# Hybrid encoder trunk on one core: the mixer's VectorE work in source order with paced convolution taps, and two projections with split weights in three passes

## The chip, the cores and the metric

The kernel runs on one core of a Trainium2 chip. The metric is the device time of one execution in microseconds; lower is better. Three runs of the kernel before took 1212.13, 1212.34 and 1212.96 us, so the median is 1212.34 us. Six units of the core appear below: TensorE (PE; its weight loads are listed as PEld), VectorE (DVE), ScalarE (ACT), GpSimd (POOL), SyncE (SP), whose queue issues the weight loads, and the DMA engines.

## The reference

Two layers act on 256 tokens of 1024 channels in f32. Each layer is a feed-forward half step, a mixer of two parallel branches (windowed attention and a convolution), a second feed-forward half step, and a gated embedding:

```python
for i in range(DEPTH):
    h = x + 0.5 * swiglu(rms_norm(x, norm_ffn1[i]), w_ffn1_in[i], w_ffn1_out[i])
    u = rms_norm(h, norm_mix[i])
    q, k, v, c, g = jnp.split(u @ w_in[i], splits, axis=-1)
    q = rms_norm(q.reshape(B, S, N_HEADS, HEAD_DIM), q_norm[i])
    k = rms_norm(k.reshape(B, S, KV_HEADS, HEAD_DIM), k_norm[i])
    y_attn = window_attention(q, k, v, sink[i], rel_bias) @ w_attn_out[i]
    c_val, c_gate = jnp.split(c, 2, axis=-1)
    c = c_val * jax.nn.sigmoid(c_gate)
    c = depthwise_conv(c, conv_w[i], conv_b[i])          # 31 taps, 512 channels
    c = jax.nn.silu(layer_norm(c, conv_ln_g[i], conv_ln_b[i]))
    y_conv = c @ w_conv_out[i]
    g_attn, g_conv = jnp.split(jax.nn.sigmoid(g), 2, axis=-1)
    h = h + (g_attn * y_attn + g_conv * y_conv) @ w_o[i]
    h = h + 0.5 * swiglu(rms_norm(h, norm_ffn2[i]), w_ffn2_in[i], w_ffn2_out[i])
    x = h + (p[i] @ w_pe_proj[i]) * jax.nn.sigmoid(rms_norm(h, norm_pe[i]) @ w_pe_gate[i])
```

Attention has 8 query heads and 2 key heads of 64 channels, a sink logit and a bias table; with 256 tokens there are two query blocks of 128.

## The kernel before

**Weights.** All weight matrices are streamed once, through one object, `Weights` (L46 to L139). A *unit* is one or two loads on SP's queue into one of five `raw` buffers of up to 1 MB. A *spec* is a piece of two row blocks of 128 by 512 columns (or four by 256). To prepare a spec, `prep_upto` casts it on ScalarE to `w_hi` (L104), and VectorE subtracts to get `w_lo` (L105): the "split". There are eight buffers of each. `get()` hands out the next spec; before it does, it runs the hooks that `later(n, fn)` has put at this place, and prepares all specs up to seven ahead (`LOOK`).

**Three passes.** A product with a split weight is made by `mm3` (L303) of three float32r matmuls: high by high, high by low, low by high (L310 to L312). A spec that was registered with `raw_spec` isn't split: `get` returns the raw f32 data, and `mm3` issues one f32 matmul (L306), which stands in the trace with two records. Only the attention and convolution outputs, `attn_out` and `conv_out`, are of this kind. While such specs wait, `limit` keeps further loads back.

**Chunks.** `chunk` (L320) runs through the specs of one accumulator in PSUM, of which there are three. After its first `get` it flushes `pending`, the evacuation of the chunk before. Two smaller PSUM tiles serve transposes.

**The mixer's stages**, `mix` from L562, in the order of the source: two chunks of the convolution's input (`conv_in`, 4 `get`s each), queries (4), keys and values (2), four chunks of gates (4 each), `attn_out` (two chunks of 2), `conv_out` (two of 2); then `w_o` in `update` (two of 4). The `get`s of a mixer are numbered from 0 in this text: 8 to 11 are the queries, 12 and 13 keys and values, 14 to 29 the gates, 30 to 33 `attn_out`, 34 to 37 `conv_out`.

- `conv_in` gates its input by a sigmoid (L594, L595); its `turn_c` transposes the result into a padded buffer and then issues the convolution: 31 taps for each of 4 channel blocks. The first tap of a block is on ScalarE (L577), the other 30 are on VectorE (L581), each adding into `y`.
- `head_norms` (L625) normalizes queries and keys: a square on ScalarE, a sum, a reciprocal root of eleven small VectorE instructions (`rsqrt`, L372), and four multiplications (L647). `turn_q` and `turn_k` transpose the results (L672, L697); they are hooks four and three `get`s later.
- The attention itself is a list of hooks among the gates (L768): `scores` (four matmuls, four reductions with bias on VectorE, four exponentials, a reciprocal, four scalings), `attend` (transposes) and `gather` (two matmuls; the second head group's evacuation, L765, writes `o`).
- `ln_by_token` (L810) transposes the finished `y` and normalizes it on VectorE; `ln_by_channel` (L829) transposes back and applies Silu on ScalarE. The result `y` feeds `conv_out`.

**What sets the order.** The kernel gives no order by hand. A planner puts the instructions of each engine in a fixed order, with a model of their times, and prefers low priority numbers, which grow along the source. Three things shift them. `with_urgency` and `high_priority` lower them by 300. In the mixer, splits get 100 more (`WEIGHTS_LAG`, set in `ws.lag`). A tap gets a number of its own, 800 behind the start of the mixer and four per tap (`BACKGROUND`), so that taps are filling work on VectorE: the planner takes one where nothing with a lower number is ready by its model.

## Time and profile before

| | |
|---|---|
| median of three runs | 1212.34 us |
| the profiled execution, its own time | 1212.65 us |
| its span in the profile | 1210.9 us |
| TensorE busy | 1155.3 us (95%) |
| VectorE busy | 736.9 us (61%) |
| ScalarE busy | 583.2 us (48%) |
| mean DMA rate | 167 GB/s |
| mean granted TensorE clock | 0.977 |

The page gives busy times of the engines, the span in 40 slices of some 30 us, the chain of work that ended last, and groups of instructions by source line. Further views used below are the waits (who waited for whom), busy times in chosen windows, and the timeline, whose rows are start, duration, engine, line, operation, written tile and read tiles, shape and number; in square brackets stands the idle time ahead of an instruction and what ended it. A matmul's end is modelled, so starts are used for steps on TensorE. The mixers lie at about 203 to 370 us and 801 to 968 us of the span.

### The profile page before, as it was taken

The page shows a single profiled execution, that of the slowest core. Times are in us where ns is not written, and L with a number is a line of the kernel's source. Part 1 is how long each engine was busy: PE and PEld are TensorE (multiplying, and loading weights), DVE is VectorE, ACT ScalarE, POOL GpSimd, SP SyncE. Part 2 cuts the span into 40 slices and gives each one's busy share as a digit, 9 for nine tenths or more (in the row PEclk, how much of TensorE's full clock was granted, in tenths as well). Part 3 has the DMA queues.
Part 4 walks back from the last instruction along what each step waited for, and adds up shares of the span by engine and source line. Part 5 has one row for each costly group of instructions (what it writes and reads, how often), then busy time and mean ns, then how long its engine had stood idle before and what let it go on. Part 6 is the DMA issues. An engine that isn't in the chain of part 4 may idle for free.

```text
span 1210.9 us, 13444 instructions
## 1 busy us (share of the span) xinstructions
PE 1155.3 (95%) x5074; PEld 906.0 (75%) x5074; DVE 736.9 (61%) x1187; ACT 583.2 (48%) x803; POOL 5.7 (0%) x21
## 2 busy tenths in 40 slices
PE   8999999949999999999999999999399999999998
PEld 6878888836647888888878888888276588888786
DVE  7555554799546655555675555557994375555544
ACT  7444444525734544444555544446177255445432
POOL 0000000000000000000000000000000000000000
PEclk9999999978999999999999999999699999999999
DMA  9866555551354565555646555565323546555520
GB/s 318 275 207 213 180 170 186 182 137 35 105 164 157 180 189 188 158 190 173 209 150 198 182 183 191 176 195 162 94 70 104 173 151 200 180 183 178 178 87 35
DMA packets 155356, 202.47 MB, mean 167 GB/s; under 512 B 5283, under 2 KB 108787, under 8 KB 155292
## 3 DMA queue, kind: packets, MB, share of 16 engines
q1 hardware_dynamic: 154204, 200.57, 52.4%
q10 hardware_dynamic: 1088, 1.05, 0.3%
q8 instruction: 40, 0.66, 0.2%
q14 instruction: 24, 0.20, 0.1%
HBM read 200.53 MB, written 1.06 MB: 166 GB/s over the span
## 4 chain that ended last, share of the span: by engine, by line
PE 90%; DVE 7%; issue 1%; ACT 1%; DMA 1%; ACTq 0%; DVEq 0%
PE ps_gu L310 13%; PE ps_gu L312 13%; PE ps_gu L311 13%; PE ps_up L310 8%; PE ps_up L311 8%; PE ps_up L312 8%; DVE y L581 4%; PE ps_co L306 2%; PE ps_g L310 2%; PE ps_ao L306 2%; PE ps_g L311 2%; PE ps_g L312 2%; PE ps_h L521 2%; PE ps_s L718 2%; PE ps_x L358 1%; PE ps_pe L312 1%
## 5 line engine op out<-in xcount | busy, mean ns | idle before, releaser
L105 DVE TENSOR_TENSOR w_lo<-raw,w_hi 128x1024 fp32r<-128x1024 f32 x360 | 439.6, 1224 | 356.9 <-ACT w_hi L104 356.3
L104 ACT CAST w_hi<-raw 128x1024 fp32r<-128x1024 f32 x360 | 376.6, 1051 | 412.9 <-PE ps_gu L312 202.9
L311 PE MATMUL ps_up<-w_lo,hh 128*128 128x512 f32 x352 | 139.4, 396 | 0.0
L312 PE MATMUL ps_up<-w_hi,hl 128*128 128x512 f32 x352 | 139.4, 396 | 0.0
L310 PE MATMUL ps_up<-w_hi,hh 128*128 128x512 f32 x352 | 139.3, 396 | 0.0
L581 DVE SCALAR_TENSOR_TENSOR y<-cpad,cw,y 128x256 f32<-128x256 f32 x240 | 101.7, 478 | 0.0
L312 PEld LDWEIGHTS ps_up<-w_hi,hl 128*128 128x128 f32 x352 | 66.0, 188 | 16.1
L310 PEld LDWEIGHTS ps_up<-w_hi,hh 128*128 128x128 f32 x352 | 66.0, 188 | 15.8
L311 PEld LDWEIGHTS ps_up<-w_lo,hh 128*128 128x128 f32 x352 | 66.0, 188 | 15.7
L311 PE MATMUL ps_gu<-w_lo,x0h 128*128 128x512 f32 x176 | 70.6, 401 | 0.0
L312 PE MATMUL ps_gu<-w_hi,x0l 128*128 128x512 f32 x176 | 70.2, 399 | 0.0
L312 PE MATMUL ps_gu<-w_hi,xn0l 128*128 128x512 f32 x176 | 69.1, 395 | 1.2 <-DVE xn0l L348 1.2
L310 PE MATMUL ps_gu<-w_hi,x0h 128*128 128x512 f32 x176 | 69.9, 397 | 0.0
L311 PE MATMUL ps_gu<-w_lo,xn0h 128*128 128x512 f32 x176 | 69.6, 395 | 0.0
L311 PE MATMUL ps_gu<-w_lo,xf0h 128*128 128x512 f32 x176 | 69.5, 395 | 0.0
L311 PE MATMUL ps_gu<-w_lo,xf1h 128*128 128x512 f32 x176 | 69.5, 395 | 0.0
L310 PE MATMUL ps_gu<-w_hi,xn0h 128*128 128x512 f32 x176 | 69.2, 393 | 0.0
L310 PE MATMUL ps_gu<-w_hi,xf1h 128*128 128x512 f32 x176 | 69.1, 393 | 0.0
L310 PE MATMUL ps_gu<-w_hi,xf0h 128*128 128x512 f32 x176 | 69.1, 393 | 0.0
L312 PE MATMUL ps_gu<-w_hi,xf1l 128*128 128x512 f32 x176 | 69.0, 395 | 0.0
L312 PE MATMUL ps_gu<-w_hi,xf0l 128*128 128x512 f32 x176 | 69.0, 395 | 0.0
L513 DVE SCALAR_TENSOR_TENSOR hh<-ps_gu,r_x,sg 128x256 f32<-128x256 f32 x88 | 42.1, 479 | 3.5 <-ACT sg L512 3.5
(217 smaller groups left out, 1805.7 us busy)
## 6 DMA issues: line engine op xcount, KB each, us to landing
raw<-in_w_ffn_in_dram SPq DMA_DIRECT2D x172, 512.0 KB
raw<-in_w_ffn_out_dram SPq DMA_DIRECT2D x40, 1024.0 KB
raw<-in_w_in_dram SPq DMA_DIRECT2D x22, 1024.0 KB
raw<-in_w_in_dram SPq DMA_DIRECT2D x16, 512.0 KB
raw<-in_w_o_dram SPq DMA_DIRECT2D x8, 1024.0 KB
raw<-in_w_pe_gate_dram SPq DMA_DIRECT2D x8, 1024.0 KB
raw<-in_w_ffn_out_dram SPq DMA_DIRECT2D x8, 512.0 KB
raw<-in_w_attn_out_dram SPq DMA_DIRECT2D x8, 512.0 KB
```

What stands on the lines that cost most here:

```text
L104: nc.scalar.copy(out=hv[:, :, d0 : d0 + w], in_=src),
L105: nc.vector.tensor_tensor(out=lv[:, :, d0 : d0 + w], in0=src, in1=hv[:, :, d0 : d0 + w].bitcast(F32), op=ALU.subtract,),
L306: nc.tensor.matmul(ps, x[:, kx, tok(t)], w[0][:, k, :], start=first, stop=last)
L310: nc.tensor.matmul(ps, xh, wh[:, k, :], start=first, stop=False)
L311: nc.tensor.matmul(ps, xh, wl[:, k, :], start=False, stop=False)
L312: nc.tensor.matmul(ps, xl, wh[:, k, :], start=False, stop=last)
L358: nc.tensor.transpose(v[:, f, i * P : (i + 1) * P], src[:, t, (k0 + f) * P : (k0 + f + 1) * P], ident)
L513: nc.vector.scalar_tensor_tensor(out=hh[:, t, :], in0=acc[:, t, 256:], scalar=x.rt(t), in1=sg, op0=ALU.mult, op1=ALU.mult)
L521: nc.tensor.transpose(ps[:, f, tok(t)], hh[:, t, f * P : (f + 1) * P], ident)
L581: nc.vector.scalar_tensor_tensor(out=y[:, i, :], in0=src, scalar=w, in1=y[:, i, :], op0=ALU.mult, op1=ALU.add)
L718: nc.tensor.matmul(ps[:, c, :], qT[v * HD : (v + 1) * HD, c, qb * P : (qb + 1) * P], kT[v * HD : (v + 1) * HD, :], start=True, stop=True,)
```

## The change

The constants `BACKGROUND` and `WEIGHTS_LAG` and their use go. In the mixer, VectorE's instructions are put in the order of the source (`manual_schedule` for VectorE alone, from the start of `mix` until just ahead of `update`); the other engines keep the planner's order. `turn_c` issues the first tap of each block at once and appends the other 30 to a list, and each `get` of the mixer issues some from it, behind its splits: three until the gates begin, and from then on five if the `get` has made a split and eight if not. `ln_by_token` issues what is left.

The specs of `attn_out` and `conv_out` become ordinary ones. Both inputs are therefore split too: `o` becomes a pair, written by a cast and a subtraction in `gather`, and `y`, after Silu, is split into `yp`, in the space of the queries' tiles, two channel blocks at a time. `split` is the helper at L345: a ScalarE cast and a VectorE subtraction. Both products then go the three-pass way of `mm3`.

```diff
--- before.py
+++ after.py
@@ -36,8 +36,6 @@
 N = 512
 LOOK = 7
 RAW_BUFS = 5
-BACKGROUND = 800
-WEIGHTS_LAG = 100
 ATTN = 5
 W_BUFS = 8
 DOWN_TAIL = 3
@@ -53,7 +51,8 @@
         self.units, self.specs = [], []
         self.raw, self.ready, self.held, self.hooks = {}, {}, {}, []
         self.next_load = self.next_prep = self.next_get = 0
-        self.rest, self.pin, self.lag = 0, None, 0
+        self.rest, self.pin = 0, None
+        self.splits, self.each = 0, None
 
     def unit(self, k, n, sources):
         self.units.append((k, n, sources))
@@ -113,6 +112,7 @@
                     for ins in parts:
                         self.pin(ins)
                     self.pin = None
+            self.splits += 1
             self.ready[self.next_prep] = (hv, lv)
             self.next_prep += 1
 
@@ -131,11 +131,11 @@
         self.hooks = [h for h in self.hooks if h[0] > i]
         for fn in due:
             fn()
-        p0 = self.tc.cur_priority
-        self.tc.cur_priority = p0 + self.lag
+        n = self.splits
         self.prep_upto(i + LOOK - self.rest)
-        self.tc.cur_priority = p0
         self.next_get += 1
+        if self.each:
+            self.each(self.splits > n)
         return self.ready.pop(i)
 
 
@@ -261,11 +261,9 @@
                 (lambda v: v[HD : 2 * HD], src[1]),
             ])
             for i in range(0, KC, 2):
-                ws.raw_spec(u, i, 2, N)
+                ws.spec(2, N, [(u, i, 0, 0, N)])
         for c in range(2):
-            u = ws.unit(KC, N, [(whole, rows_of(a["w_conv_out"][l], 0, KC, c * N, N))])
-            for i in range(0, KC, 2):
-                ws.raw_spec(u, i, 2, N)
+            block(a["w_conv_out"][l], 0, KC, c * N)
         for c in range(2):
             for k0 in (0, 4):
                 block(a["w_o"][l], k0, 4, c * N)
@@ -562,13 +560,20 @@
     def mix(l, st, nxt):
         u = st.x
         cw, kg, bias, sink = (late[n] for n in ("cw", "kg", "bias", "sink"))
-        with tc.tile_pool(name="mix_pool", bufs=1) as mp:
+        with tc.tile_pool(name="mix_pool", bufs=1) as mp, ExitStack() as order:
+            order.enter_context(tc.manual_schedule(engines={mybir.EngineType.DVE}))
             cpad = mp.tile([P, KC, T + 2 * PAD], F32, name="cpad", tag="cpad")
             nc.gpsimd.memset(cpad[:, :, 0:PAD], 0.0)
             nc.gpsimd.memset(cpad[:, :, PAD + T :], 0.0)
             y = mp.tile([P, KC, T], F32, name="y")
-            background = tc.cur_priority + BACKGROUND
-            ws.lag = WEIGHTS_LAG
+            taps, rate = [], [3, 3]
+
+            def some_taps(split):
+
+                for _ in range(min(len(taps), rate[0 if split else 1])):
+                    taps.pop(0)()
+
+            ws.each = some_taps
 
             def tap(i, t):
                 src = cpad[:, i, t : t + T]
@@ -602,12 +607,9 @@
                             for t in range(NT):
                                 nc.tensor.transpose(ps[:, f, tok(t)], cc[:, t, f * P : (f + 1) * P], ident)
                         nc.scalar.copy(out=cpad[:, i : i + 2, PAD : PAD + T], in_=ps)
-                        p0 = tc.cur_priority
-                        for t in range(TAPS):
-                            for f in range(2):
-                                tc.cur_priority = background + KC * t + i + f
-                                tap(i + f, t)
-                        tc.cur_priority = p0
+                        for f in range(2):
+                            tap(i + f, 0)
+                        taps.extend(lambda t=t, f=f: tap(i + f, t) for t in range(1, TAPS) for f in range(2))
 
                     ws.later(1, turn_c)
 
@@ -703,7 +705,7 @@
             keys_values()
 
 
-            o = mp.tile([P, GROUP, T], F32, name="o")
+            o = parts(mp, GROUP, "o")
             sc = {}
             o_ps = {}
 
@@ -762,7 +764,7 @@
                     )
                 if v == 1:
                     ov = o_ps.pop(qb).rearrange("p (c q) -> p c q", c=GROUP)
-                    nc.scalar.copy(out=o[:, :, tok(qb)], in_=ov[:, :, ::-1])
+                    split([p[:, :, tok(qb)] for p in o], ov[:, :, ::-1])
 
 
             for at, fn in (
@@ -790,6 +792,7 @@
                     gs = g[:, t, c * N : (c + 2) * N]
                     tc.keep_in_program_order(nc.scalar.activation(out=gs, in_=gs, func=AF.Sigmoid))
 
+            rate[:] = 5, 8
             for c in range(4):
                 gates(c)
 
@@ -805,9 +808,15 @@
                 chunk(acc, KC, o)
                 pending.append(evac)
 
+            yp = (
+                mp.tile([P, KC, T], F32R, name="y_h", tag="sqq"),
+                mp.tile([P, KC, T], F32R, name="y_l", tag="qT"),
+            )
             yn = mp.tile([P, NT, N], F32, name="yn", tag="pTs", bufs=2)
 
             def ln_by_token():
+                while taps:
+                    taps.pop(0)()
                 for t in range(NT):
                     ps = tr_tile("ps_yt")
                     for i in range(KC):
@@ -837,6 +846,7 @@
                             out=y[:, i + f, :], in_=ps[:, f, :], func=AF.Silu,
                             scale=pcol("conv_ln_g", l, i + f), bias=pcol("conv_ln_b", l, i + f),
                         )
+                    split([p[:, i : i + 2, :] for p in yp], y[:, i : i + 2, :])
 
             ws.later(2, lambda: with_urgency(ln_by_token))
             attn_out(0)
@@ -876,7 +886,7 @@
 
             for c in range(2):
                 acc = acc_tile("ps_co")
-                chunk(acc, KC, y, 2 if c else 0, after=lambda t: urgent(t, 1, acc))
+                chunk(acc, KC, yp, 2 if c else 0, after=lambda t: urgent(t, 1, acc))
                 if c == 0:
                     pending.append(lambda acc=acc: [merge(t, 0, acc) for t in range(NT)])
                     ws.later(2, lambda: [turns.pop(0)() for _ in range(2)])
@@ -887,7 +897,8 @@
                 xs = x_tok[:, t, cols(c)]
                 nc.vector.tensor_tensor(out=xs, in0=acc[:, t, :], in1=xs, op=ALU.add)
 
-            ws.lag = 0
+            order.close()
+            ws.each = None
             return update(nxt(), KD, (Halves(ym[0]), Halves(ym[1])), add, 2)
 
 
```

## The prediction

> **What bounds the kernel now.** I read the page's busy table and slices first, then the waits, then the busy time of the mixer by stages, then single rows there.
>
> ```profile
> PE 1155.3 (95%) x5074; PEld 906.0 (75%) x5074; DVE 736.9 (61%) x1187; ACT 583.2 (48%) x803; POOL 5.7 (0%) x21
> PE   8999999949999999999999999999399999999998
> DVE  7555554799546655555675555557994375555544
> PEclk9999999978999999999999999999699999999999
> ```
>
> TensorE sets the pace everywhere except in two slices, the ninth and the twenty-ninth, one per layer. There VectorE is full (9) and TensorE is not (4 and 3). Both lie in the mixer.
>
> ```profile
> PE ps_qt L672 <- DVE qn L647: 16.4, 1, 16.4
> PE ps_qt L672 <- issue: 16.4, 1, 16.4
> PE ps_kt L697 <- DVE kn L647: 5.8, 2, 2.9
> ```
> ```profile
> core 0: us, PE busy (x) PEld busy (x) DVE busy (x) ACT busy (x) POOL busy (x), PEclk, DMA share, GB/s
> 252.88:275.55 22.67, 2.83 (x12) 1.80 (x11) 22.67 (x72) 4.39 (x8) 0.00 (x0) 0.58 0.38 94
> 275.55:283.76 8.21, 8.21 (x19) 6.03 (x20) 8.21 (x26) 2.50 (x6) 0.00 (x0) 0.50 0.00 0
> 206.74:365.70 158.96, 136.63 (x554) 94.87 (x553) 116.18 (x284) 79.72 (x129) 2.55 (x6) 0.91 0.42 127
> 805.09:962.72 157.63, 136.31 (x554) 94.55 (x553) 116.04 (x284) 79.74 (x129) 2.23 (x6) 0.91 0.42 128
> ```
>
> In each layer TensorE stands 16.4 us before the transposes of the normalized queries and 2.9 before those of the keys. Of 22.67 us it works 2.83. Then comes a clock cost: for 8.21 us it is busy all the time at a granted clock of 0.50, which loses half of that, **4.1 us**. The stretch that I calculate runs from the last-but-one transposes of the input to the last-but-one of the merged branches: 158.96 and 157.63 us, mean **158.3**.
>
> Why the queries are late is seen in VectorE's own rows:
>
> ```profile
> 265.79 0.15 DVE L381 SCALAR_TENSOR_TENSOR rh<-nwt,rh 128x4 f32<-128x4 f32 x1
> 265.86 0.88 DVE L581 SCALAR_TENSOR_TENSOR y<-cpad,cw,y 128x256 f32<-128x256 f32 x2
> 266.66 0.17 DVE L381 SCALAR_TENSOR_TENSOR rh<-nwt,rh 128x16 f32<-128x16 f32 x1
> 274.35 6.42 DVE L581 SCALAR_TENSOR_TENSOR y<-cpad,cw,y 128x256 f32<-128x256 f32 x16
> 280.68 0.48 DVE L727 CUSTOM_DVE_ANT_0 s<-ps_s,bias,sink 128x256 f32<-128x256 f32 x1
> ```
>
> Between any two short steps of the reciprocal root stand two taps of the convolution, 0.87 us a step. Two such chains of twelve steps, queries' and keys', take turns: about 21 us for what takes 2.4 us each when uninterrupted (below). A tap in a row of 16 costs (280.68 - 274.35)/16 = **0.396 us**.
>
> **The change part by part.** *Order of the source.* In the source the norms stand in one piece, behind what the same `get` has issued: one split, then three taps (five from the gates on). The stall of 19.3 us goes, but VectorE can no longer run ahead. At the first evacuation of the convolution's input it waits for TensorE, and from there it is one line up to the layer norm by token, before which all taps must be done. I sum that line.
>
> ```profile
> L105 DVE TENSOR_TENSOR w_lo<-raw,w_hi 128x1024 fp32r<-128x1024 f32 x31 | 37.6, 1223 | 12.6 <-ACT w_hi L104 12.4
> L727 DVE CUSTOM_DVE_ANT_0 s<-ps_s,bias,sink 128x256 f32<-128x256 f32 x16 | 6.8, 484 | 2.8 <-PE ps_s L718 2.8
> L595 DVE SCALAR_TENSOR_TENSOR hh<-ps_c,r_x,sg 128x256 f32<-128x256 f32 x4 | 1.9, 482 | 1.6 <-ACT sg L594 1.6
> L647 DVE TENSOR_TENSOR qn<-ps_q,rh 128x256 f32<-128x256 f32 x4 | 1.4, 420 | 0.0
> L636 DVE TENSOR_REDUCE ms<-qn 128x16 f32<-128x1024 f32 x1 | 1.2, 1217 | 0.0
> ```
> ```profile
> 325.44 0.70 DVE L816 BATCH_NORM_STATS2 six<-ps_yt 128x6 f32<-128x512 f32 x1 [1.98 <-PE ps_yt L814]
> 326.39 0.15 DVE L820 TENSOR_SCALAR mv<-mv 128x1 f32<-128x1 f32 x1
> 328.77 0.81 DVE L824 TENSOR_SCALAR yn<-ps_yt,mv,rs 128x512 f32<-128x512 f32 x1
> 329.55 2.36 DVE L105 TENSOR_TENSOR w_lo<-raw,w_hi 128x1024 fp32r<-128x1024 f32 x2
> ```
>
> Two splits in a row take 2.36, one 1.22, so a split's step is 1.14. A layer norm of one token half takes 329.55 - 325.44 = 4.1, and the uninterrupted root in it 328.77 - 326.39 = 2.4. The line: splits for the `get`s 4 to 30, 27 x 1.14 = 30.8 (the last eight are the new ones of `attn_out` and `conv_out`); 120 taps, 47.5; gating, 1.9; the norm of the queries 1.2 + 2.4 + 1.4 and of the keys about 3.4 (same chain, shorter ends), 8.4; scores 6.8 and four reciprocals of 0.1; the new split of `o`, two of 0.6 (half of a 1024 split), 1.2; two layer norms 8.2. Together **105.2 us**.
>
> *What it waits for.* A reciprocal now stands directly behind its four scores and must wait for ScalarE's exponentials, with the next split and taps queued behind it. Before, taps filled this time; the traced distance from the end of the scores to the last exponential or to the reciprocal bounds it:
>
> ```profile
> 299.26 1.67 DVE L581 SCALAR_TENSOR_TENSOR y<-cpad,cw,y 128x256 f32<-128x256 f32 x4
> 309.89 1.22 DVE L105 TENSOR_TENSOR w_lo<-raw,w_hi 128x1024 fp32r<-128x1024 f32 x1
> 316.02 0.18 DVE L738 RECIPROCAL den<-den 128x4 f32<-128x4 f32 x1 [2.17 <-ACT s L734]
> ```
> ```profile
> 300.12 0.19 ACT L734 ACTIVATION_READ_ACCUMULATOR s<-s,nm 128x1 f32 x1
> 308.35 1.28 ACT L791 ACT_TABLE_LOAD   x1
> ```
>
> At best 300.31 - 299.26 = 1.05 us; at worst 316.02 - 309.89 = 6.1, where ScalarE had put the gates' sigmoid with its tables between. I take 2.1 each, nearer the short end, since the long one needs that intrusion: 8.3 for four (4.2 to 24.4). Add 3 for the first cast and the first turn of the convolution input, which nothing hides any more. [...]
>
> *Its start.* Before this line TensorE has 48 passes to do, 24 of them on weights and inputs of the first column half, then the first accumulator's rest.
>
> ```profile
> 318.21 0.39 PE L311 MATMUL ps_g<-w_lo,xm0h 128*128 128x512 f32 x1
> 323.42 0.39 PE L310 MATMUL ps_g<-w_hi,xm0h 128*128 128x512 f32 x1
> 337.03 11.32 PE L306 MATMUL ps_ao<-raw,o 128*128 128x512 f32 x26
> 348.19 0.93 PE L834 MATMUL ps_yc<-ident,yn 128*128 128x128 f32 x7
> 361.49 0.63 PE L358 MATMUL ps_x<-ident,g 128*128 128x128 f32 x4 [1.22 <-DVE g L870]
> ```
>
> From 318.21 to 323.42 there are 23 steps: 0.227 us a pass. 48 passes are 10.9, with transposes **12 us**. In the trace the first accumulator came at 18 because passes of the queries went ahead of it; in the new order their weights are split behind the second input turn, so I take 12 and keep 18 as bound.
>
> *Three passes for attn_out and conv_out.* A record of the single-pass form takes (348.19 - 337.03)/26 = 0.43 and each multiplication has two records, 0.86, against 3 x 0.227 = 0.68. 16 multiplications a projection: 13.8 becomes 10.9, so 2.9 each. For `attn_out` this is free TensorE time; for `conv_out`, behind the line, it counts in full: 10.9 plus 0.5 of transposes and the 1.0 to 1.2 wait for the merge, **12.4**.
>
> ```profile
> 348.72 1.93 ACT L836 ACTIVATE y<-ps_yc,par 128x256 f32<-128x256 f32 x4 [7.77 <-PE ps_yc L834]
> 362.16 0.59 ACT L347 CAST ym_h<-ps_x 128x512 fp32r<-128x512 f32 x1 [11.50 <-PE ps_x L358]
> L104 ACT CAST w_hi<-raw 128x1024 fp32r<-128x1024 f32 x360 | 376.6, 1051 | 412.9 <-PE ps_gu L312 202.9
> ACT w_hi L104 <- DMA raw<-in_w_o_dram: 5.6, 3, 3.2
> ```
>
> Ahead of it stand transposes (0.5), half of the four Silu (1.0), and newly a cast and a subtraction for half of `y` (0.6 each): **2.7**. ScalarE gets eight more casts of 1.05 and two of 0.6 a layer, the two evacuations of `o` only change their type, on 79.7 us of work over 159: no bound.
>
> *The rest at nothing.* Loads are the same ones on SP's queue; only the rule that held them back behind unsplit weights no longer acts. DMA runs at 0.42 of its share here, and the splits' lead of seven `get`s covers a late load; if that cover were gone the casts would wait as they do for `w_o` now, 5.6 us in both layers. The reused tiles of queries are dead two stages earlier. POOL's copies of the sink wait for their tiles as before.
>
> *Sum for a layer.* 12 + 105.2 + 8.3 + 3 + 2.7 + 12.4 = 143.6. TensorE has 136.6 us of busy records there, 4.1 of them lost to half clock and 5.8 to the longer passes; it is the faster one and now idles ahead of the layer norm, so I charge a cold spell of 4.1: **147.7** against 158.3, 10.6 less, 21 in two layers. The profiled execution took 1212.65 us (its span 1210.9), 0.3 over the median of 1212.34: 1212.65 - 21.2 = **1191**. [...]
>
> **The rivals.**
> *VectorE waits little and TensorE stays warm.* Reciprocals at 1.05, no cold spell: 12 + 105.2 + 4.2 + 3 + 2.7 + 12.4 = 139.5, so 18.8 a layer: **1175**. If all waits hid, 132.3 a layer: 1161. For it: three of four reciprocals in the trace have ScalarE nearly free. Against: the line still leaves TensorE some 17 us idle (143.6 - 136.6 + 5.8 + 4.1), which must then fall in short pieces.
> *Slower: the ordered queue is blocked at the reciprocals.* Each takes the traced 6.1 because the sigmoids or casts get ahead on ScalarE, 24.4, the split behind each waits a further 1.05 for its late cast, 4.2, and the start stays at 18: 18 + 105.2 + 24.4 + 4.2 + 3 + 2.7 + 12.4 + 4.1 = 174, or 168 with the early start: 10 to 16 a layer, **1232 to 1244**. It decides from 22 us of waits a layer (158.3 - 12 - 105.2 - 2.7 - 12.4 - 4.1), where I have 11.3. Against: half of those waits needs the rare intrusion.
> *The order changes nothing*: taps still cut the norms apart and the stall stays. Then only the projections count, 5.8 less 1.2 for the new cast and subtraction: 4.6 a layer, **1203**. Against: all VectorE work of the mixer lies inside the ordered block.
> *A draw*: the start at 18 and waits of 14 to 16 us give 156.4 to 158.4 with the spell: **1209 to 1213**.
>
> **How the numbers follow.** Forecast 0.48, quick rival 0.18, unchanged order 0.10, draw 0.11, slower 0.13. The likeliest's own range is 1180 to 1203. Eight in ten must reach the quick case and the draw, and a light form of the blocked queue: 1164 to 1217. 0.2% (2.4 us) is about what a measurement tells from no change. Faster: 0.48 + 0.18 + 0.10 and half of the draw's weight, 0.81; same 0.06; slower 0.13.
>
> **What would show it.** Right: no idle before the query transposes above 2 us; short root steps back to back; taps ending only just before the layer norm, VectorE above nine tenths through the gates; the waits naming ACT at the reciprocal; TensorE's idle now ahead of `ps_yt`, `ps_yc` or `ps_co`. Wrong: TensorE idle under 8 us in the stretch (quick), a VectorE idle of over 22 us before the taps end (slower), or taps still between root steps.

## The result and the profile after

The changed kernel takes **1232.38 us** (median of four runs, 1231.76 to 1232.59); the kernel before, run beside it, 1212.24. The ratio is 1.0166 with a 95% interval of 1.0148 to 1.0183: 20 us slower. The prediction said 1191 us, range 1164 to 1217, and gave "slower" a chance of 0.13. The time went the other way and lies 15 us above the range.

The page of the changed kernel, its busy times and three of its rows of 40 slices:

```profile
PE 1158.4 (94%) x5138; PEld 924.6 (75%) x5138; DVE 764.6 (62%) x1211; ACT 597.2 (49%) x819; POOL 3.7 (0%) x21
PE   8999999969858999999999999999796889999998
DVE  7655554687866655555675555557879675555444
PEclk9999999979979999999999999999798899999999
```

The single hole of before (a 4 and a 3 in TensorE's row) is gone. In each layer a shallower one is spread over five slices (6 9 8 5 8, and 7 9 6 8 8), and the clock's row now dips twice per layer where it dipped once. VectorE has 27.7 us more work than before (736.9).

The waits of TensorE in the first layer's mixer up to conv_out (who waited, for whom: total us, times, longest):

```profile
PE ps_yc L843 <- DVE yn L833: 7.6, 2, 4.2
PE ps_kt L699 <- DVE kn L649: 7.4, 1, 7.4
PE ps_yt L823 <- DVE ol L346: 2.3, 1, 2.3
...
PE ps_qt L674 <- issue: 1.6, 1, 1.6
```

The 16.4 us ahead of the query transposes became 1.6. The keys' wait grew from 2.9 to 7.4, and new waits stand at the layer norm. What VectorE waited for in the same part:

```profile
DVE den L740 <- ACT s L736: 11.6, 4, 4.0
...
DVE y L586 <- ACT y L582: 5.7, 1, 5.7
DVE hh L600 <- ACT sg L599: 3.6, 3, 1.9
...
DVE six L825 <- PE ps_yt L823: 1.7, 1, 1.7
```

Busy times by stretches show where the time went; the columns are start and end, length, PE, PEld, DVE, ACT and POOL busy with the number of records, granted clock, DMA share, GB/s. First after, then before:

```profile
220.37:345.98 125.61, 105.37 (x459) 79.23 (x457) 101.89 (x252) 70.26 (x115) 0.38 (x2) 0.90 0.40 122
206.14:349.56 143.42, 121.36 (x533) 92.28 (x531) 116.23 (x280) 81.46 (x132) 1.44 (x6) 0.90 0.39 118
196.69:349.56 152.87, 130.81 (x574) 99.93 (x572) 119.49 (x283) 85.34 (x137) 1.44 (x6) 0.90 0.39 118
349.56:398.50 48.94, 42.17 (x177) 32.74 (x177) 30.04 (x36) 18.41 (x27) 0.00 (x0) 0.92 0.46 145
398.50:525.01 126.51, 125.69 (x576) 103.00 (x574) 73.51 (x94) 60.59 (x77) 0.00 (x0) 1.00 0.57 180
```
```profile
197.29:349.82 152.53, 131.41 (x558) 96.00 (x557) 113.87 (x278) 82.17 (x132) 2.55 (x6) 0.91 0.41 125
349.82:390.52 40.70, 39.48 (x157) 26.77 (x156) 21.05 (x28) 13.39 (x22) 0.00 (x0) 1.00 0.49 151
390.52:516.43 125.91, 125.91 (x580) 103.50 (x578) 74.38 (x94) 61.71 (x79) 0.00 (x0) 1.00 0.57 180
```

Two stretches recur below. The **way** runs from the first pass of `conv_in` to the first of `conv_out`; the **stage** from there to the first pass of the second feed-forward step. The way is as long as before: 152.9 against 152.5 us. The stage grew by 8.2, from 40.7 to 48.9, in both layers. So the change won nothing ahead of conv_out and lost behind it. Layer by layer: way +0.3 and +1.8, stage +8.2 and +8.1, the feed-forward's first stretch +0.6 each, 19.7 us before rounding; 0.6 were won ahead of the first mixer, and the span is 19.0 longer (1229.9 against 1210.9).

### The profile page after: what moved, and what is told of

Its sections match the earlier page's. It is cut to its first block, busy times and chain, and to the rows that moved or that the text cites. A ratio compares the mean times of both kernels' runs of the same rounds, so it can differ in the third digit from the quotient of the medians.

```text
span 1229.9 us, 13639 instructions
## 1 busy us (share of the span) xinstructions
PE 1158.4 (94%) x5138; PEld 924.6 (75%) x5138; DVE 764.6 (62%) x1211; ACT 597.2 (49%) x819; POOL 3.7 (0%) x21
## 4 chain that ended last, share of the span: by engine, by line
PE 87%; DVE 10%; ACT 2%; issue 1%; DMA 0%; SPq 0%; DVEq 0%; ACTq 0%
PE ps_gu L310 13%; PE ps_gu L308 13%; PE ps_gu L309 13%; PE ps_up L308 8%; PE ps_up L310 8%; PE ps_up L309 8%; DVE w_lo L104 3%; DVE y L586 3%; PE ps_g L308 2%; PE ps_h L519 2%; PE ps_s L720 2%; PE ps_g L309 1%; PE ps_g L310 1%; PE ps_pe L310 1%; PE ps_pe L309 1%; PE ps_pe L308 1%
## 5 line engine op out<-in xcount | busy, mean ns | idle before, releaser
L104 DVE TENSOR_TENSOR w_lo<-raw,w_hi 128x1024 fp32r<-128x1024 f32 x376 | 458.5, 1223 | 341.2 <-ACT w_hi L103 341.1
L103 ACT CAST w_hi<-raw 128x1024 fp32r<-128x1024 f32 x376 | 393.5, 1050 | 474.5 <-PE ps_gu L310 201.1
L345 ACT CAST hh<-ps_h 128x512 fp32r<-128x512 f32 x44 | 25.8, 586 | 40.2 <-PE ps_h L519 40.2
```

The source lines that it names most:

```text
L103: nc.scalar.copy(out=hv[:, :, d0 : d0 + w], in_=src),
L104: nc.vector.tensor_tensor(out=lv[:, :, d0 : d0 + w], in0=src, in1=hv[:, :, d0 : d0 + w].bitcast(F32), op=ALU.subtract,),
L345: nc.scalar.copy(out=hi, in_=src)
```

## The experiments

Three theories. **A:** in conv_out's stage, source order puts weight splits ahead of the merges (L879, L880), and these splits wait for casts that wait for `w_hi` buffers. **B:** the split weights by themselves cost more than the three passes save. **C:** the order by itself is the harm, whatever the weights; the blocked queue of the prediction's slower rival, VectorE's waits ahead of conv_out, is one form of it.

All times are medians, the ratio is to the kernel before, run beside each on the same chip; way and stage are given for layer 0 and layer 1.

| kernel | us | ratio (95% interval) | way | stage |
|---|---|---|---|---|
| before | 1212.2 | | 152.5, 151.1 | 40.7, 40.8 |
| after | 1232.4 | 1.0166 (1.0148 to 1.0183) | 152.9, 152.9 | 48.9, 48.9 |
| split only | 1221.4 | 1.0080 (1.0065 to 1.0095) | 153.3, 157.1 | 41.0, 41.4 |
| order only | 1220.4 | 1.0073 (1.0057 to 1.0088) | 152.3, 151.9 | 43.5, 45.0 |
| order ended early | 1217.9 | 1.0051 (1.0036 to 1.0066) | 154.5, 154.5 | 41.2, 41.2 |
| reciprocals behind | 1227.9 | 1.0133 (1.0116 to 1.0150) | 149.8, 150.8 | 49.9, 48.9 |
| both of these | 1210.7 | 0.9990 (0.9981 to 0.9999) | 151.3, 151.1 | 40.4, 40.8 |
| order up to the scores | 1230.3 | 1.0152 (1.0135 to 1.0169) | 160.7, 160.7 | 40.8, 40.8 |
| merges first | 1221.5 | 1.0076 (1.0061 to 1.0091) | 153.4, 152.8 | 43.7, 43.0 |
| both, low part of o behind | 1210.1 | 0.9986 (0.9976 to 0.9995) | 150.7, 150.8 | 40.3, 40.8 |
| that, first taps later | 1206.0 | 0.9951 (0.9937 to 0.9965) | 149.8, 148.8 | 40.8, 40.5 |
| both, fp32 weights | **1198.1** | 0.9888 (0.9874 to 0.9903) | 144.8, 144.9 | 40.8, 40.8 |
| that, conv_out split | 1212.5 | 1.0008 (0.9998 to 1.0017) | 151.9, 150.2 | 41.7, 40.3 |
| that, attn_out split | 1205.8 | 0.9955 (0.9940 to 0.9970) | 147.3, 146.8 | 42.0, 42.0 |

### The two parts of the change apart

Split weights and three passes alone, in the planner's order:

```diff
--- before.py
             for i in range(0, KC, 2):
-                ws.raw_spec(u, i, 2, N)
+                ws.spec(2, N, [(u, i, 0, 0, N)])
...
-            o = mp.tile([P, GROUP, T], F32, name="o")
+            o = parts(mp, GROUP, "o")
...
+                    split([p[:, i : i + 2, :] for p in yp], y[:, i : i + 2, :])
...
-                chunk(acc, KC, y, 2 if c else 0, after=lambda t: urgent(t, 1, acc))
+                chunk(acc, KC, yp, 2 if c else 0, after=lambda t: urgent(t, 1, acc))
```

> The kernel before with only the split weights and the three passes in attn_out and conv_out; the planner's order, its lag and its taps in the background stay. Theory A (the loss is made by source order and split weights together: splits that wait for buffers stand ahead of the merges of conv_out): without the source order the stage from conv_out to the second FFN stays near the 40.7 us of before, and 128 matmuls of 0.86 us per layer that become 384 of 0.227 us are paid in part by 16 more splits on VectorE: 1195 to 1215 us. Rival B (the split weights by themselves cost more than they save: more casts, more subtractions, a ring of eight held by more owners): at or above the changed kernel's 1232, and the stage at 46 us or more.

The order alone is the changed kernel with these edits taken back.

> The changed kernel with fp32 weights and single fp32 passes in attn_out and conv_out as before; only VectorE's source order and the paced taps remain. Theory A: the eight conv_out weight tiles no longer hold ring buffers, so no split ahead of the merges waits, and the stage is within 2 us of 40.7; the time is 1205 to 1220, by what the front stretch does. Rival C (the order alone does the harm, whatever the weights): stage 46 us or more in each layer, and 1228 to 1245 us in all.

(The counts in the first expectation are too high: it is 32 fp32 products per layer that become 96 passes.) Measured: 1221.4 and 1220.4 us. Each part alone makes the kernel slower, by 9.8 and 8.8 us, and the two add up to 18.6 of the 20. The split-only time lies in neither forecast: above A's 1215, below B's 1232. The split-only kernel's windows, layer 0, and one of TensorE's waits on its way:

```profile
196.70:349.98 153.28, 128.49 (x574) 98.55 (x572) 121.03 (x287) 85.34 (x137) 2.50 (x6) 0.90 0.40 124
349.98:390.94 40.96, 39.12 (x172) 31.03 (x173) 25.37 (x32) 17.12 (x25) 0.00 (x0) 0.95 0.48 149
```
```profile
PE ps_co L308 <- ACT y_h L345: 4.9, 1, 4.9
```

On the way TensorE has 2.9 us less to do than before (128.5 against 131.4), as the prediction's sum had it, and VectorE 7.2 more (121.0 against 113.9); the way is no shorter. In the stage the three passes should save another 2.9, yet it is 0.3 longer: the granted clock was 0.95 where it was 1.00. TensorE waits 4.9 us at conv_out's first pass for the new cast of `y` (4.0 in the second layer), where the kernel before waits at most 1.3 us between the keys' transposes and that pass. So B holds in direction: the loss is there with the old order. In the order-only kernel the stage is 43.5 and 45.0, more than the 42.7 that A allowed for raw weights and less than C's 46; this run does not decide between them. Its loss, too, lies behind conv_out's start: the stages grew by 2.8 and 4.2, the ways by -0.2 and 0.8. Why the split-only kernel's way grew by 6.0 in the second layer and 0.8 in the first was not followed.

### The order in conv_out's stage

VectorE's, ScalarE's and one of TensorE's rows of the changed kernel there (start, duration, engine, line, operation, what it waited for):

```profile
360.14 1.23 DVE L104 TENSOR_TENSOR w_lo<-raw,w_hi 128x1024 fp32r<-128x1024 f32 x1 [2.74 <-ACT w_hi L103]
361.29 0.68 DVE L879 TENSOR_TENSOR g<-ps_co,g 128x512 f32<-128x512 f32 x1
...
371.69 1.23 DVE L104 TENSOR_TENSOR w_lo<-raw,w_hi 128x1024 fp32r<-128x1024 f32 x1 [3.27 <-ACT w_hi L103]
372.84 0.68 DVE L879 TENSOR_TENSOR g<-ps_co,g 128x512 f32<-128x512 f32 x1
```
```profile
355.09 1.05 ACT L103 CAST w_hi<-raw 128x1024 fp32r<-128x1024 f32 x1 [5.07 <-PE ps_co L310]
359.06 1.05 ACT L103 CAST w_hi<-raw 128x1024 fp32r<-128x1024 f32 x1 [2.91 <-PE ps_co L310]
```
```profile
362.84 0.63 PE L356 MATMUL ps_x<-ident,g 128*128 128x128 f32 x4 [2.65 <-DVE g L880]
```

A cast waits for a conv_out pass to release its buffer, the split waits for the cast, the merge stands behind the split, and TensorE stands 2.65 us before the merge's transposes. In the first two of the following kernels this is changed. In the first the written order ends before the loop, so that the planner places the merges; the second keeps the merges in source order but issues no split in the loop (the four splits follow behind the end of the written order). The third leaves the stage alone and moves the reciprocals.

```diff
--- after.py (order ended early)
+            order.close()
+            ws.each = None
             for c in range(2):
                 acc = acc_tile("ps_co")
...
-            order.close()
-            ws.each = None
             return update(nxt(), KD, (Halves(ym[0]), Halves(ym[1])), add, 2)
--- after.py (merges first)
         while done < n_k:
+            if done == 0 and first:
+                flush()
...
+            ws.rest = 4
             for c in range(2):
                 acc = acc_tile("ps_co")
-                chunk(acc, KC, yp, 2 if c else 0, after=lambda t: urgent(t, 1, acc))
+                chunk(acc, KC, yp, 2 if c else 0, after=lambda t: urgent(t, 1, acc), first=c == 1)
...
+            for n in range(1, 5):
+                ws.later(n, lambda n=n: setattr(ws, "rest", 4 - n))
--- after.py (reciprocals behind)
-                nc.vector.reciprocal(out=den, in_=den)
-                for c in range(GROUP):
...
+                behind.append(weigh)
...
                 for _ in range(min(len(taps), rate[0 if split else 1])):
                     taps.pop(0)()
+                while behind:
+                    behind.pop(0)()
```

> The changed kernel with the written order of VectorE ended, and the taps' hook taken away, just ahead of conv_out's loop, so that the planner places the merges, the splits and the turns of that stage. Theory A: the merges come ahead of the waiting splits, conv_out's last 12 passes come before w_o's first, and the stage falls from 48.9 to 41 to 43 us in both layers: 1213 to 1218 us. Rivals (B, the work of the splits; or the cold clock at conv_out's start, which is set earlier): stage at 47 to 49, time 1228 to 1234 us.

> The changed kernel in source order throughout, but in conv_out's loop no weight tile is split ahead (the four splits are made two per fetch from w_o's first fetch on), and the first branch's merge is flushed ahead of the second chunk's fetch. No wait and no work is taken out, only the order on VectorE changes. Theory A (the splits that stand ahead of the merges do it): the stage from conv_out to the second FFN falls from 48.9 to 41 to 44 us, 1214 to 1221 us. Rival (it takes the planner's freedom, or w_o's passes now wait for their late splits): 46 to 50 us, 1227 to 1234.

> The changed kernel with the reciprocal of the softmax sum and the scaling of the exponentials issued behind the split and the taps of the same weight fetch, instead of ahead of them; all else in source order. If VectorE's line sets the start of conv_out, the four waits of 3.1, 2.0, 2.5 and 4.0 us at the reciprocals in each layer are filled with taps, conv_out starts 8 to 11 us earlier, and the time is 1210 to 1217 us. Rival (something else sets the start, the keys' norms or PE's own passes): start within 3 us of 349.6, time 1226 to 1234.

Measured: 1217.9 with a stage of 41.2 in both layers; 1221.5 with 43.7 and 43.0; 1227.9 with stages of 49.9 and 48.9. A is confirmed for the changed kernel. The merges-first kernel decides it, because it keeps every split and the order of the merges and only takes splits from ahead of them. VectorE's rows of the merges-first kernel, its first stage, and the first stage of the kernel whose order ended early:

```profile
357.85 1.22 DVE L104 TENSOR_TENSOR w_lo<-raw,w_hi 128x1024 fp32r<-128x1024 f32 x1 [2.54 <-ACT w_hi L103]
360.74 0.69 DVE L881 TENSOR_TENSOR g<-ps_co,g 128x512 f32<-128x512 f32 x1 [1.66 <-PE ps_co L310]
```
```profile
350.57:394.27 43.70, 40.89 (x177) 32.09 (x177) 29.65 (x36) 18.41 (x27) 0.00 (x0) 0.93 0.52 162
```
```profile
350.91:392.13 41.22, 39.60 (x172) 31.39 (x173) 27.66 (x34) 17.13 (x25) 0.00 (x0) 0.94 0.55 174
```

A split issued ahead of the loop still waits 2.54 us, but the first merge no longer waits for it: it stands another 1.66 us for TensorE's own passes, and TensorE's idle time in the stage falls from 6.8 us (48.94 - 42.17) to 2.8. Of the 8.2 us lost, 5.2 and 5.9 come back; the planner takes most of what is left (1.6 us idle in its stage), though that kernel's way is 1.6 longer than the changed kernel's, which was not followed. The time, 1221.5, is half a microsecond above A's range.

### The waits ahead of conv_out

The reciprocals' four waits are 11.6 us per layer. Moved behind the taps, they gave back 4.5 us in all, 3.1 and 2.1 on the way, not the 8 to 11 us per layer of the forecast; the time lies in its rival's range. The kernel's waits show why:

```profile
DVE ol L346 <- ACT oh L345: 6.9, 1, 6.9
...
DVE den L744 <- ACT s L738: 0.8, 2, 0.4
```

The reciprocals wait 0.8 instead of 11.6, and the next instruction that needs another engine, the low part of attention's output, waits 6.9 where the changed kernel's list has no such row. Both edits together:

> The changed kernel with both edits of the earlier runs: written order ended ahead of conv_out's loop, and reciprocals and scalings issued behind the split and the taps. If the two losses lie apart (the stage from conv_out on, and the waits ahead of it), the gains add: 14.5 and 4.5 us, so 1213 to 1215 us, still above before. If a stage that follows gives one of them back (a later weight load, a cold clock), 1216 to 1219.

1210.7: 21.7 us gained where 14.5 and 4.5 were to add, better than either forecast, and just ahead of before. Then the waits that were left were taken in turn, by issuing the low part's subtraction behind the taps (for the first query block, those of the next fetch), and by releasing the first VectorE taps one fetch later:

```diff
-                    split([p[:, :, tok(qb)] for p in o], ov[:, :, ::-1])
+                    nc.scalar.copy(out=oh, in_=ov[:, :, ::-1])
+                    behind.append((ws.next_get + 1 - qb, lambda: nc.vector.tensor_tensor(
+                        out=ol, in0=ov[:, :, ::-1], in1=oh.bitcast(F32), op=ALU.subtract
+                    )))
...
-                        taps.extend(lambda t=t, f=f: tap(i + f, t) for t in range(1, TAPS) for f in range(2))
+                        ws.later(2, lambda: taps.extend(
+                            lambda t=t, f=f: tap(i + f, t) for t in range(1, TAPS) for f in range(2)
+                        ))
```

> The kernel of the two edits together (order ended ahead of conv_out, reciprocals behind the taps) and one more: the subtraction that makes attention's low part waits behind the split and the taps too, for the first query block those of the next fetch; in the run before it held VectorE for one wait of 6.9 us per layer. If VectorE's waits ahead of the layer norm set conv_out's start, it comes 4 to 7 us earlier in each layer: 1197 to 1203 us. If another engine's order sets it (PE's place for the transposes of y, ScalarE's chain), 0 to 2 us per layer: 1207 to 1211.

> As the kernel with attention's low part behind, and the first VectorE taps of each channel pair come one fetch later than their ScalarE tap, for which they waited 5.7 us once per layer. If VectorE's line sets conv_out's start, 2 to 5 us per layer earlier than there; if not, within 1 us per layer of it.

The first is a miss for the line theory, and its rival's range holds: 1210.1, the way 0.3 to 0.7 us shorter. Its waits of VectorE:

```profile
DVE six L839 <- PE ps_yt L837: 3.2, 1, 3.2
DVE ol L779 <- ACT oh L778: 2.6, 1, 2.6
```

The wait for attention's low part fell from 6.9 to 2.6, and 3.2 us of waiting for TensorE's `ps_yt` appeared. The second edit gave 4.1 us in all, and the way became 0.8 and 2.0 us shorter, one layer in each of its two forecasts; the wait that it was made for fell only from 5.7 to 4.5. VectorE's waits were real, but most of each only moved on to the next place where engines meet.

### The cut-up norms, made worse

One kernel kept raw weights and source order up to the first scores only, then gave all remaining taps to the planner, at background priority.

```diff
--- after.py, raw weights
+            def planner_from_here():
+                order.close()
+                ws.each, ws.lag = None, 100
+                p0 = tc.cur_priority
+                while taps:
+                    t, i = taps.pop(0)
+                    tc.cur_priority = background + KC * t + i
+                    tap(i, t)
+                tc.cur_priority = p0
```

> Raw weights and single passes as before; VectorE in source order with three taps per fetch only from conv_in to the first scores, from there the planner's order with the rest of the taps in the background, as before. The query transposes then wait 2 us and not 16. Theory D (the planner's cut-up head norms cost PE time that nothing later takes back): the way from conv_in to conv_out falls from 152 to 140 to 147 us in both layers and the time is 1194 to 1206. Rival E (VectorE's work ahead of conv_out sets that point, so a stall that goes at the norms comes back at the taps): 150 to 154 us, time 1208 to 1216.

1230.3, neither theory's number, for the kernel did not do what it was made for. Its VectorE rows and TensorE's waits:

```profile
252.12 1.21 DVE L645 TENSOR_REDUCE ms<-qn 128x16 f32<-128x1024 f32 x1
...
256.64 0.17 DVE L382 TENSOR_TENSOR nwt<-rh 128x16 f32<-128x16 f32 x1
256.73 0.87 DVE L593 SCALAR_TENSOR_TENSOR y<-cpad,cw,y 128x256 f32<-128x256 f32 x2
257.52 0.17 DVE L383 SCALAR_TENSOR_TENSOR nwt<-nwt,ms 128x16 f32<-128x16 f32 x1
```
```profile
PE ps_kt L706 <- DVE kn L656: 15.3, 1, 15.3
PE ps_qt L681 <- issue: 13.4, 1, 13.4
```

The taps, issued later in the source and bound by no order, slid forward between the steps of the root: the queries' norm takes 13.8 us (252.12 to 265.87, when the next split starts behind the four multiplications) instead of the 5.2 of the changed kernel. TensorE stands 28.7 us at the two transposes, against 19.3 in before, and the way is 8 to 10 us longer. The stall grew by 9.4 and the way by 8.2 and 9.6, which fits a stall that is not taken back later. It is not shown, for the taps moved too, and the changed kernel, whose two waits are some 10 us shorter than before's, has no shorter way. D and E stay undecided.

### The split weights, one projection at a time

The kernel of both edits, with raw weights and single fp32 passes in both projections, and then with split weights in one of the two (the diffs are those of the first experiment, taken back).

> The kernel of the two edits together, with fp32 weights and single fp32 passes in attn_out and conv_out as before. VectorE has some 11 us less per layer ahead of conv_out and no low part of attention to wait for, PE some 2.9 us more on each side of conv_out's start. If VectorE's line sets that start, it comes 5 to 9 us earlier and the time is 1197 to 1206: the split weights cost more than the three passes save. If PE's or ScalarE's order sets it, 0 to +3 us per layer: 1209 to 1217.

> The fastest kernel so far (order ended ahead of conv_out, reciprocals behind, fp32 weights) with split weights and three passes in conv_out alone. Four more splits of 1.2 us per layer and the split of y (two subtractions of 0.65 us) come on VectorE ahead of conv_out's last passes, PE saves 16 times 0.18 us. If split weights cost by VectorE's share, 5 to 7 us in all lost against it: 1202 to 1206. If conv_out alone gains as the prediction had it, 1192 to 1197.

> The same with split weights and three passes in attn_out alone. Four more splits per layer and attention's two low parts, one of which held VectorE for 6.9 us in an earlier run. By VectorE's share: 1203 to 1208. If attention's low part is no cost there: 1196 to 1200.

Without split weights 1198.1 us, the fastest of all: 1.1% faster than before, and within the forecast for the case that VectorE's line sets conv_out's start. So the source order is a gain once its two blocked places are mended, and split weights take 12.5 us of it (1210.7 - 1198.1), 6.5 and 6.1 of them on the way.

The two traces show how. With raw weights the taps end at 319.0, and the layer norm runs while TensorE still has 28 records of attn_out to do (from 325.96). With split weights the taps end at 336.0, when attn_out is done; TensorE then stands 8.7 and 8.5 us per layer at `ps_yc`, waiting for the norm, a wait that the raw kernel's list does not have. A half-clock spell of 10.2 and 13.7 us follows there, which the raw kernel does not have either; TensorE's work in it is 5.0 and 6.2 us, so an estimated 2.5 and 3.1 us are lost to it.

Attention's projection alone takes 7.7, within its forecast. conv_out's alone takes 14.4, above both of its forecasts and more than both projections together, and not by VectorE's load. Rows around the layer norm, first with raw weights (TensorE, then VectorE), then with conv_out split (the same):

```profile
323.59 0.38 PE L829 MATMUL ps_yt<-ident,y 128*128 128x128 f32 x2
325.47 0.66 PE L829 MATMUL ps_yt<-ident,y 128*128 128x128 f32 x4 [1.49 <-ACT o L777]
325.96 9.61 PE L306 MATMUL ps_ao<-raw,o 128*128 128x512 f32 x22
```
```profile
307.79 11.17 DVE L590 SCALAR_TENSOR_TENSOR y<-cpad,cw,y 128x256 f32<-128x256 f32 x28
```
```profile
326.78 0.55 PE L831 MATMUL ps_yt<-ident,y 128*128 128x128 f32 x3 [1.60 <-ACT o L775]
327.17 8.75 PE L304 MATMUL ps_ao<-raw,o 128*128 128x512 f32 x20
335.75 0.38 PE L831 MATMUL ps_yt<-ident,y 128*128 128x128 f32 x2
```
```profile
322.24 0.49 DVE L588 SCALAR_TENSOR_TENSOR y<-cpad,cw,y 128x256 f32<-128x256 f32 x1
336.06 0.70 DVE L833 BATCH_NORM_STATS2 six<-ps_yt 128x6 f32<-128x512 f32 x1 [13.34 <-PE ps_yt L831]
```

With conv_out split VectorE had its taps done at 322.7 and then stood 13.3 us. The first layer norm can start only when its transposes of `y` are complete, and the last two of these stand in TensorE's fixed order behind 20 records of attn_out. With raw weights all stand ahead of the 22 records, though the taps end only 3.8 us earlier (319.0). That the planner moved them because its model saw the taps end later is likely, but was not tried by itself. The kernel with both projections split has no wait for `ps_yt` in its list, so this stand belongs to the conv_out kernel alone, and the two projections' costs do not add.

## Why the prediction was wrong

**"Three passes ... 2.9 each ... for conv_out, behind the line, it counts in full."** TensorE's share is right (its busy time on the way fell 2.9 in the split-only kernel), but the price is larger than the gain. Split weights cost 9.8 us in the planner's order, 12.0 in source order (after against order only) and 12.5 with the mended order. The forecast's own sum holds such a price: eight splits (9.1), the two of `o` (1.2) and the cast and subtraction of `y` (1.2) are 11.5 us per layer ahead of conv_out, against 2.9 saved behind its start. By its own terms the projections lost 17 us in two layers, and the prediction never drew this balance. Where it did forecast them by themselves, in the third rival (planner's order), it put the splits at nothing and got a gain of 4.6 per layer, 1203 us. There the sign failed: 1221.4 was measured.

**"The rest at nothing."** This is the step that put the time above before. The sum ends at the second of four groups of merged transposes (it calls it the last but one), and the stage behind it was in no term and in no rival. The third and fourth groups start at 380.4 and 384.0, where before they started at 366.9 and 370.4. Source order there puts splits that wait for buffers ahead of merges for which TensorE waits: the stage costs 8.2 us more per layer, of which 5 to 6 are shown to come from splits ahead of merges. The prediction asked what stands behind a waiting reciprocal, and did not ask it of a waiting split, although it quoted the waits of splits for casts and casts for TensorE in before.

**The line's waits, "8.3 for four" and "3 for the first cast and the first turn".** Mis-sized. Measured 11.6 for the reciprocals (3.1, 2.0, 2.5 and 4.0) and 7.6 for the first tap and the second gating (5.67 and 1.94), and 1.7 more at `ps_yt`. VectorE's busy time in the line, 101.9 us in 125.6, with 2.8 of small gaps between, is right: 104.7 against 105.2. With VectorE's first gating 14.2 us after the stretch's start instead of 12, and 3.6 instead of 2.7 behind the line, conv_out starts 143.4 us after the stretch's start instead of 131.2. That is 12.2 more per layer.

From there to the second group of merged transposes (366.02) it is 16.5 instead of 12.4, another 4.1: an estimated 2.2 for half clock up to 353.90, 1.5 for the longer wait for the merge (2.65), the rest not followed. The rest of the stage and 0.6 of the feed-forward add 8.2. Less the 4.1 that the sum charged for a cold clock, the forecast of 10.6 less per layer missed by 20.4, which makes 9.8 more, as measured.

**"A cold spell of 4.1."** Mis-sized as well. Before had one half-clock spell of 27.3 us per layer, with 11.0 us of TensorE's work in it in the first; the changed kernel has four, 37.5 us, with 22.1 us of work, of which half, 11.1, is lost by estimate (its conv_out passes start 0.43 us apart at a granted 0.50, 350.57 to 353.56, and 0.23 apart at 1.00, 354.20 to 356.29). Only part of it lies where TensorE sets the pace: two steps of 3.41 us in the stage, full of work (350.49 to 353.90 and 364.14 to 367.56), cost an estimated 3.4.

**What was right.** The stall at the queries is gone, the root's steps stand in one piece, and TensorE's idle moved to `ps_yt`, `ps_yc` and `ps_co`, though the keys' transposes, which the list of signs left out, wait as long (7.4) as `ps_yc` (7.6). VectorE was not above nine tenths through the gates: its row has 8, 7 and 8 there. The core of the idea holds too: with raw weights and the two blocked places mended, source order gives 14 us. That is less than the 21 forecast for the whole change, and it needed two edits that the change did not have. The changed kernel's rows show the blocking that the prediction's line counts on: the split behind each of the first layer's four reciprocals started 0.09 or 0.10 us behind it (277.60 behind 277.51, 284.44 behind 284.34, 298.06 behind 297.97, 310.08 behind 309.98), and the merge at 372.84, whose product had its last pass started by 359.79, came only behind the split at 371.69, ahead of which VectorE had stood idle for 3.27 us.

**The rival that named the time.** "Slower: the ordered queue is blocked at the reciprocals" gave 1232 to 1244, and 1232.4 came. Its mechanism did not carry it: the reciprocals waited 11.6 and not 24.4, and moving them gave 4.5 us. Its mark, over 22 us of VectorE idle before the taps end, was narrowly missed: some 21 from the line's start at 220.37 to the taps' end at 336.31. That the number came is luck: a blocked queue it was, but most of the loss against before stands at the merges. The order-only kernel comes nearer to this rival, with 17.0 us of waits at the reciprocals; what moving them alone is worth there was not run.

## What to carry to other kernels

When an engine's order is fixed by hand, walk through all of its queue up to the last instruction under that order, and ask of each one that can wait (a split for a buffer as much as a reciprocal for a sum) who needs what stands behind it. Where TensorE waits for VectorE anyway, see what faster passes on TensorE bring: in the split-only kernel's first layer TensorE had 2.9 us less to do on the way, VectorE 7.2 more, and the way was no shorter. Test the parts of a change apart: here one part was a gain of 1.1% once mended, and the other was a loss in every combination that was run.

## What the runs showed of the hardware

In the mixers of before and of the changed kernel the half-clock spells came in steps of one length, 3.41 us. Of the changed kernel's stretches (columns as above; the granted clock is the third number from the end):

```profile
251.51:254.92 3.41, 1.58 (x8) 0.87 (x8) 3.06 (x13) 2.21 (x3) 0.00 (x0) 1.00 0.39 150
254.92:258.33 3.41, 1.05 (x6) 0.65 (x4) 3.41 (x6) 1.17 (x2) 0.00 (x0) 0.50 0.00 0
...
265.16:268.57 3.41, 3.41 (x9) 2.29 (x8) 3.41 (x8) 0.00 (x0) 0.00 (x0) 0.50 0.00 1
268.57:271.98 3.41, 3.41 (x9) 2.64 (x9) 3.41 (x8) 0.00 (x0) 0.00 (x0) 0.50 0.82 198
271.98:275.40 3.42, 3.42 (x15) 2.40 (x14) 2.43 (x11) 2.33 (x3) 0.00 (x0) 1.00 0.56 109
...
326.60:330.01 3.41, 3.04 (x8) 2.46 (x9) 3.41 (x8) 0.00 (x0) 0.00 (x0) 0.50 0.64 250
```

The spells of the first layer's mixer last 17.07, 3.41, 13.65 and 3.42 us, that is 5, 1, 4 and 1 times 3.41, and those of the second layer's have the same numbers of steps; before has one spell of 27.3 us, 8 steps, in each layer. A step at full clock in which TensorE was busy for 1.58 of 3.41 us (46%), not idle, was followed by half clock. A step at half clock with 3.04 busy was followed by full clock (326.60 to 330.01). But 265.16 to 268.57, busy throughout, was followed by another step at half clock, and full clock came only behind that one. In it ran the scores, eight matmuls from 264.56 on, which use 64 of the 128 rows (`64*128` in their row, where the gates' passes have `128*128`); whether that is the cause was not tried.
